# Alternating the column halves of a pair's values, keeping norm chains whole, and idle matmuls in a two-block fp32 kernel

## The chip, the cores and the metric

The kernel runs on one core of one Trainium2 chip. Five engines work in parallel, each with its own instruction stream: TensorE (PE, matmuls; its weight loads are shown apart as PEld), VectorE (DVE), ScalarE (ACT), GpSimd (POOL) and SyncE (SP), which issues most DMAs. TensorE's clock has two levels, 1.2 and 2.4 GHz; the profile shows the granted clock as a share of the full one. The metric is the device time in microseconds of one execution, lower is better, compared as medians of several runs.

## The reference

Two transformer blocks of two layers each work on 256 latent tokens and 256 context tokens of width 1024, in fp32. All of it is matrix products, norms and modulations of this kind:

```python
def ffn_half_step(h, shift, scale, gate, g, w_in, w_out):
    a, b = jnp.split(modulate(rms_norm(h, g), shift, scale) @ w_in, 2, axis=-1)
    return h + FFN_RESIDUAL_WEIGHT * gate * ((jax.nn.silu(a) * b) @ w_out)

# first block, each layer: ffn, mixer1, ffn
q = mla_queries(q_lat, g_q_lat[l], w_q_up[l], g_q_head[l], rope)
k, v = mla_keys_values(kv_lat, k_pe, g_kv_lat[l], w_kv_up[l], g_k_head[l], rope)
kc, vc = mla_keys_values(kv_lat_c, k_pe_c, g_kv_lat[l], w_kv_up[l], g_k_head[l], None)
attn = latent_attention(q, k, v, kc, vc)          # softmax(q k' + ...) v, 8 heads
sg = spatial_gating(sg_in, g_sgu[l], w_spatial[l], b_spatial[l])
cv = short_conv(cv_in, w_conv[l])
h = h + mod_l[5] * merge_groups(attn, sg, cv, g_out[l], w_mix_out[l])

# second block, each layer: mixer2 (an mLSTM group and a neighbourhood attention), then
def sq_relu_mlp(h, w1, w2):
    return jnp.square(jax.nn.relu(h @ w1)) @ w2
```

`mla_queries` and `mla_keys_values` norm a latent (384 or 256 wide), multiply it up to 8 heads of 96, norm each head and rotate 32 of its values. Latent queries attend to all 512 tokens, context queries to the 256 context tokens alone. The last layer of each block needs latent outputs only. Shift, scale and gate come from products of the condition vectors with large modulation weights.

## The kernel before, in words

Activations lie features on partitions: `h[k]`, k = 0 to 7, holds 128 features of 512 tokens, columns 0 to 255 latent (stream 0), 256 to 511 context (stream 1). Each fp32 operand is split into a high and a low part, and each product is three matmuls: high by high, high by low, low by high (`mm_feat`, L340 to L342, tokens as columns; `mm_tok`, L354 to L356, tokens as rows). Weights come in pieces of 1 MB by DMA into three buffers; ScalarE rounds them to the high part (`wh`, L310), VectorE subtracts for the low one (`wl`, L311). Modulation sums (`ad`, L473 and L475) are background work on VectorE: calls of `bg` hand them out, and their weights too come by DMA into these buffers.

The instructions' order on each engine is not the order in the text alone: a planner simulates the program and orders each engine's instructions by its own estimates of when they become due. `issue_after(ins)` limits it: instructions made inside it come behind `ins` where they are on the same engine as `ins`.

A norm has four stages. `Sumsq.add` collects squares feature tile by feature tile as the residual is written: ScalarE squares (L98), VectorE adds (L100), the last tile is squared by VectorE (L103) and kept as a second sum. `rstd_cols` sums over features with narrow matmuls (L552) and runs a chain of eleven small VectorE instructions for the inverse root: L563, L565, then three times two of L570 and one of L571. `rstd_rows` (L546) spreads the factors over partitions by two matmuls. `tile` applies them: VectorE (L133), ScalarE for the high part (`xnh`, L596), VectorE for the low part (`xnl`, L597).

mixer1 makes the latents, norms those of queries (`qs`) and then of keys and values (`kvs`) by `rms_split`, and then multiplies up the queries (L1023, psum `qu`, two halves), keys and values (psum `kvu`). Rotated keys (`kraw`, L873 on VectorE) and queries are transposed per head (psum `tr`, L1135) ahead of attention.

`attention` is a generator over steps, one for each head and query tile of 128: 16 steps per stream. A step makes scores (L807), the row maximum on VectorE (L813), the exponential on ScalarE (L815), the inverse sum and the scaling on VectorE (L817, L818). Three steps later come the transposes of the probabilities (L828), copied by ScalarE (L829) into `pT`, and at each even step the values (L838) of a whole head, for both query tiles: 4 key tiles for latent queries, 2 for context ones. A head's output takes 64 of 128 partitions of a psum tile, so its matmuls use one half of the array's columns (`tile_position=(0, 64 * j)`, j = 0 or 1), and the next head's the other. One fp32 matmul here is two instructions in the trace. Between the steps other generators put in the spatial gating (psum `vs`, L1112, the same kind of halves) and parts of the output projection. mixer2's neighbourhood attention uses the same generator with a bias.

In the second block's mlp, `block` makes three pieces at once at the edge (when both streams are there): `project` multiplies all of stream 0 and then stream 1, ScalarE takes the relu out of psum (L1660), VectorE squares it (L1661) and makes the low part (L594), and `bg` adds modulation sums.

Of the kernel before, what the change touches and what calls it, by code (L numbers as in the profile page):

```python
# [13 lines left out]
ALU = mybir.AluOpType  # L14
AX = mybir.AxisListType

P = 128
D = 1024
KT = 8
# [59 lines left out]
class Sumsq:  # L79


    def __init__(self, b, streams):
        self.b = b
        self.streams = streams
        self.accs = {}

    def add(self, s, k):

        if s not in self.streams:
            return  # L90
        b, nc = self.b, self.b.nc
        ap = b.h[k][:, 256 * s : 256 * s + 256]
        if k == 0:
            self.accs[s] = [b.acc()]
            nc.scalar.activation(self.accs[s][0], ap, AF.Square)
        elif k < KT - 1:
            sq = b.sqtmp()
            nc.scalar.activation(sq, ap, AF.Square)  # L98
            acc = self.accs[s][0]
            nc.vector.tensor_tensor(acc, acc, sq, op=ALU.add)  # L100
        else:
            sq = b.sqtmp()
            nc.vector.tensor_tensor(sq, ap, ap, op=ALU.mult)  # L103
            self.accs[s].append(sq)


class Norm(Sumsq):
# [9 lines left out]
    def emit(self, s):  # L117
        b = self.b
        if s not in self.streams:
            return  # L120
        rb = b.rstd_bc(self.accs[s], D)
        if self.gs is None:
            b.need(self.key, self.sh_chunk)
            b.need(self.key, self.sc_chunk)
            self.gs = b.make_gs(self.key, self.sc_chunk, *self.gain)
        for k in range(KT):
            self.tile(s, k, rb)
# [102 lines left out]
class Builder:  # L230
# [99 lines left out]
    def mm_feat(self, ps, w, m0, x, c0, c1, ks, first, last, kw0=0, m=P):  # L330
        nc = self.nc
        ks = list(ks)
        o = ps[:m, : c1 - c0]
        for i, k in enumerate(ks):
            kw = k - kw0
            st = first and i == 0
            en = last and i == len(ks) - 1
            wh = w.h[:, kw, m0 : m0 + m]
            wl = w.l[:, kw, m0 : m0 + m]
            nc.tensor.matmul(o, wh, x.H(k, c0, c1), start=st, stop=False)  # L340
            nc.tensor.matmul(o, wh, x.L(k, c0, c1), start=False, stop=False)  # L341
            nc.tensor.matmul(o, wl, x.H(k, c0, c1), start=False, stop=en)  # L342


    def mm_tok(self, ps_ap, w, n0, n1, x, t0, ks, first, last, kw0=0):
# [90 lines left out]
    SG0 = 2  # L436
    SG1 = 2
    ML_B = 4

    def ada_tasks(self, blk, l):  # L440

# [92 lines left out]
            v.scalar_tensor_tensor(t, t, -0.5, y, op0=ALU.mult, op1=ALU.mult)  # L534
            v.scalar_tensor_tensor(y, t, 1.5, y, op0=ALU.add, op1=ALU.mult)

    def rstd_bc(self, accs, n):


        return self.rstd_rows(self.psum("nm", "nm"), accs, n)  # L540

    def rstd_rows(self, ps, accs, n):
        nc = self.nc
        y = self.rstd_cols(ps, accs, n)
        for b in range(2):
            self.rows_done = nc.tensor.matmul(ps[:, b * P : (b + 1) * P], y[:, b : b + 1].broadcast_to([P, P]), self.ident, start=True, stop=True)  # L546
        return ps[:, 0:256]

    def token_sums(self, ps, sq, first, last):

        for b in range(2):
            self.nc.tensor.matmul(ps[:, 256 + b : 257 + b], sq[:, b * P : (b + 1) * P], self.onecol,  # L552
                                  start=(first and b == 0), stop=(last and b == 1))

    def rstd_cols(self, ps, accs, n):

        nc = self.nc
        v = nc.vector
        for i, acc in enumerate(accs):
            self.token_sums(ps, acc, i == 0, i == len(accs) - 1)  # L560

        m = self.small(2, "ms", tag="ns")
        v.tensor_scalar(m, ps[:, 256:258], -0.5 / n, -0.5 * EPS, op0=ALU.mult, op1=ALU.add)  # L563
# [3 lines left out]
        for _ in range(3):  # L567
            for b in range(2):
                c = slice(b, b + 1)
                v.scalar_tensor_tensor(t[:, c], y[:, c], m[:, c], y[:, c], op0=ALU.mult, op1=ALU.mult)  # L570
            v.scalar_tensor_tensor(y, t, 1.5, y, op0=ALU.add, op1=ALU.mult)  # L571
        return y

    def sumsq(self, tiles):
# [118 lines left out]
    def ffn(self, l, which, streams, x, nxt, side=None, start=None):  # L693
        nc = self.nc
# [46 lines left out]
        def first_pair():  # L741

            raws = [start.load(0)]
            ws = weights(0)
            raws += [start.load(i) for i in range(1, 4)]
            pp = [[self.psum("fa") for _ in ws] for _ in range(2)]
            for i in range(4):
# [44 lines left out]
    def attention(self, units, nring):  # L792

        nc = self.nc
        ring = [self.arena([P, 2, 1024], F32, "att") for _ in range(nring)]
        st = [(i, qt) for i in range(len(units)) for qt in range(2)]
# [30 lines left out]
            nc.scalar.activation(pT[:, :nk, qt * P : (qt + 1) * P], pt[:, : nk * P].rearrange("p (k q) -> p k q", q=P), AF.Copy)  # L829
            live[i] = pT  # L830

        def values(i):
            q_ap, k_ap, v_ap, po, j, s, bias, done = units[i]
            nk, k0 = (4, 0) if s == 0 else (2, 2)
            pT = live.pop(i)
            o = po()
            for k in range(nk):
                nc.tensor.matmul(o, v_ap(k0 + k), pT[:, k, :], start=(k == 0), stop=(k == nk - 1), tile_position=(0, 64 * j))  # L838
            if done is not None:
                done()  # L840

        n = len(st)
        for e in range(n + 6):
            if e < n:
                scores(*st[e])
            if 3 <= e < n + 3:
                transposes(*st[e - 3])
            if e >= 6 and (e - 6) % 2 == 0 and (e - 6) // 2 < len(units):
                values((e - 6) // 2)
            yield  # L850


# [39 lines left out]

    def rms_split(self, tiles, n, gcol, dst, k0, streams):

        nc = self.nc
        for s in streams:
            c0, c1 = 256 * s, 256 * s + 256
            rb = self.rstd_bc(self.sumsq([t[:, c0:c1] for t in tiles]), n)
            for i, t in enumerate(tiles):
                u = self.ntmp("ru")  # L900
                nc.vector.scalar_tensor_tensor(u, t[:, c0:c1], gcol[:, i : i + 1], rb, op0=ALU.mult, op1=ALU.mult)
                self.split_from(u, dst, k0 + i, c0, c1)

    def mixer1(self, l, last, x, nxt):
        nc = self.nc
# [60 lines left out]
        self.rms_split([kvl[:, i, :] for i in range(2)], 256, self.vec("g_kv_lat", 2 * l, 2), kvs, 0, [0, 1])  # L966


        vgz = self.arena([P, 2048], F32, "vgz")
# [50 lines left out]
        for half in range(2):  # L1020
            w = self.weight(a["w_q_up"][l][:, half * 384 : half * 384 + 384], 3, 384)
            for tt in tts:
# [5 lines left out]
                nc.scalar.activation(sq, ps[:, :384], AF.Square)  # L1028
                o = tt * 8 + 4 * half
                v.tensor_reduce(qss[:, o : o + 4], sq.rearrange("p (h d) -> p h d", d=96), axis=AX.X, op=ALU.add)  # L1030
        kflat, kraw = zip(*[heads("kraw") for _ in range(2)])
        kss = self.small(32, "kss")
        vt = self.arena([P, 4, 512], F32, "vt")
# [93 lines left out]

        qT = [self.arena([P, 4, T], F32, "qT") for _ in range(2)]
        kT = [self.arena([P, 4, T], F32, "kT") for _ in range(2)]
        for h in range(8):  # L1130
            for src, dst, n in ((kflat, kT, 4), (qflat, qT, nt)):
                ps = self.psum("tr")
# [511 lines left out]
    def mlp(self, l, streams, x, nxt):  # L1644
# [8 lines left out]
        def block(t0, edge):  # L1653
# [7 lines left out]
                nc.vector.tensor_tensor(r, r, r, op=ALU.mult)  # L1661
                self.split_from(r, g[t // 8], t % 8 + j, c0, c1)

            self.project(blocks, x, streams, n > 1, range(KT), evac)
            self.bg(n)
            return 2 * n

        def part_in(t0, t1, edge=False):
# [36 lines left out]
    def run(self):  # L1705
# [22 lines left out]
        for l in range(2):  # L1728
# [6 lines left out]
                return  # L1735
            rest = [0] if last else both
            n = norm(0, l, "g_ffn2", 6, rest)
            self.mixer1(l, last, x, n)
            x = n.x
            if self.stop == "h2":  # L1740
# [17 lines left out]
        for l in range(2):  # L1758
            last = l == 1
            rest = [0] if last else both  # L1760
            n = norm(1, l, "norm2_g_2", 3, rest)
            self.mixer2(l, last, x, n)
            x = n.x
            n = Final(self) if last else norm(1, 1, "norm1_g_2", 0, both)
# [64 lines left out]
```

## Time and profile before

| what | value |
| --- | --- |
| three runs | 2982.9, 2988.43, 2988.7 us, median 2988.43 us |
| the profiled execution's own time | 2986.06 us |
| its span in the profile | 2984.3 us |
| mean granted clock of TensorE | 0.988 |
| TensorE busy | 2903.6 us, 97% |
| VectorE busy | 2121.7 us, 71% |
| ScalarE busy | 1088.5 us, 36% |

The span is the stretch that the profile covers; 1.8 us of the execution lie around it. Start times in rows count from the start of the span. A busy share is a mean over stages that have different limits. Instructions of TensorE overlap at their ends, so the distance from start to start tells what one costs, and its duration is longer.

### The profile page before, as it was taken

The numbers are of one execution on the slowest core, as the hardware profiler recorded it, in microseconds if no ns is written. First come the engines' busy times: TensorE is split into PE (matmuls) and PEld (weight loads), VectorE is DVE, ScalarE is ACT, GpSimd is POOL, SyncE is SP. The second block draws the span as 40 slices with busy tenths as digits, with TensorE's granted clock in tenths as the row PEclk, the third lists the DMA queues.
The fourth block names the chain that finished last, engine by engine and source line by source line (L and its number), as shares of the span: only waits on it lengthen the run. The fifth ranks groups of instructions, "written<-read, shape, count | busy, mean of one in ns | idle before, by whom it ended". The sixth has DMA issues, their size and how long they took to land.

```text
span 2984.3 us, 44357 instructions
## 1 busy us (share of the span) xinstructions
PE 2903.6 (97%) x17770; PEld 2484.6 (83%) x17770; DVE 2121.7 (71%) x4323; ACT 1088.5 (36%) x1989; POOL 47.8 (2%) x83
## 2 busy tenths in 40 slices
PE   8999999999999999999988999999999999999998
PEld 6788898688888888888868999886888889995998
DVE  6978768769887697786885675437687875537665
ACT  3222135533222232222653443335342223434443
POOL 0000000000000000000000000011000000011000
PEclk9999999999999999999998999999999999999999
DMA  7655524114655446554323554202255652312453
GB/s 243 216 181 199 171 60 125 47 50 163 216 184 166 140 157 201 179 172 146 107 92 111 175 174 129 75 1 68 85 161 178 198 170 58 118 50 84 155 184 112
DMA packets 357610, 410.25 MB, mean 137 GB/s; under 512 B 24066, under 2 KB 297884, under 8 KB 357404
## 3 DMA queue, kind: packets, MB, share of 16 engines
q1 hardware_dynamic: 353512, 403.63, 41.9%
q10 hardware_dynamic: 3892, 3.78, 0.4%
q8 instruction: 140, 2.29, 0.3%
q14 instruction: 66, 0.54, 0.1%
HBM read 406.34 MB, written 1.05 MB: 137 GB/s over the span
## 4 chain that ended last, share of the span: by engine, by line
PE 91%; DVE 5%; DMA 2%; ACT 1%; issue 1%; SPq 0%; POOL 0%; ACTq 0%; DVEq 0%; POOLq 0%
PE pj L340 13%; PE pj L341 13%; PE pj L342 13%; PE fa L340 9%; PE fa L341 9%; PE fa L342 9%; PE po L838 3%; PE pf L340 2%; PE pf L342 2%; PE pf L341 2%; PE sc L807 2%; DVE wl L311 1%; PE pt L828 1%; PE pj L354 1%; PE pj L355 1%; PE pj L356 1%
## 5 line engine op out<-in xcount | busy, mean ns | idle before, releaser
L310 ACT ACTIVATE wh<-wr 128x1024 fp32r<-128x1024 f32 (+3 forms) x542 | 526.0, 1017 | 858.0 <-PE pj L341 473.3
L311 DVE TENSOR_TENSOR wl<-wr,wh 128x1024 fp32r<-128x1024 f32 (+3 forms) x542 | 624.3, 1175 | 175.3 <-ACT wh L310 173.2
L475 DVE SCALAR_TENSOR_TENSOR ad<-wr,silu,ad 128x512 f32<-128x512 f32 x784 | 548.3, 744 | 17.1 <-DMA wr<-in_w_ada_dram 17.1
L340 PE MATMUL fa<-xnh,wh 128*128 128x512 f32 (+1 forms) x1472 | 520.5, 360 | 5.8 <-ACT xnh L596 4.1
L341 PE MATMUL fa<-xnl,wh 128*128 128x512 f32 (+1 forms) x1472 | 523.1, 357 | 1.9 <-DVE xnl L597 1.9
L342 PE MATMUL fa<-xnh,wl 128*128 128x512 f32 (+1 forms) x1472 | 522.9, 356 | 1.3 <-DVE wl L311 1.3
L340 PE MATMUL pj<-gh,wh 128*128 128x256 f32 (+1 forms) x1372 | 457.2, 334 | 0.0
L342 PE MATMUL pj<-gh,wl 128*128 128x256 f32 (+1 forms) x1372 | 455.7, 333 | 0.0
L341 PE MATMUL pj<-gl,wh 128*128 128x256 f32 (+1 forms) x1372 | 455.5, 332 | 0.0
L340 PEld LDWEIGHTS fa<-xnh,wh 128*128 128x128 f32 x1472 | 275.2, 189 | 52.3 <-ACT xnh L596 5.5
L342 PEld LDWEIGHTS fa<-xnh,wl 128*128 128x128 f32 x1472 | 277.6, 189 | 45.1 <-DVE wl L311 1.7
L341 PEld LDWEIGHTS fa<-xnl,wh 128*128 128x128 f32 x1472 | 277.6, 189 | 43.7 <-DVE xnl L597 2.9
L340 PEld LDWEIGHTS pj<-gh,wh 128*128 128x128 f32 x1372 | 258.7, 189 | 28.3 <-ACT wh L310 1.6
L342 PEld LDWEIGHTS pj<-gh,wl 128*128 128x128 f32 x1372 | 258.5, 188 | 27.2
L341 PEld LDWEIGHTS pj<-gl,wh 128*128 128x128 f32 x1372 | 258.8, 189 | 26.2 <-issue 0.2
L340 PE MATMUL pj<-xnh,wh 128*128 128x256 f32 (+1 forms) x824 | 259.0, 324 | 2.4 <-ACT xnh L596 2.2
L342 PE MATMUL pj<-xnh,wl 128*128 128x256 f32 (+1 forms) x824 | 260.8, 320 | 0.0
L341 PE MATMUL pj<-xnl,wh 128*128 128x256 f32 (+1 forms) x824 | 259.4, 319 | 1.2 <-DVE xnl L597 1.1
L340 PEld LDWEIGHTS pj<-xnh,wh 128*128 128x128 f32 x824 | 155.2, 193 | 14.6 <-ACT xnh L596 3.2
L341 PEld LDWEIGHTS pj<-xnl,wh 128*128 128x128 f32 x824 | 156.5, 191 | 12.6 <-DVE xnl L597 1.4
L342 PEld LDWEIGHTS pj<-xnh,wl 128*128 128x128 f32 x824 | 156.0, 190 | 11.9
L689 DVE SCALAR_TENSOR_TENSOR h<-pj,mod,h 128x256 f32<-128x256 f32 x144 | 66.2, 479 | 109.9 <-PE pj L342 109.9
(372 smaller groups left out, 4260.9 us busy)
## 6 DMA issues: line engine op xcount, KB each, us to landing
wr<-in_w_ada_dram SPq DMA_DIRECT2D x112, 1024.0 KB, 5.2
wr<-in_w_ffn_in_dram SPq DMA_DIRECT2D x88, 1024.0 KB, 5.1
wr<-in_w_mlp_dram SPq DMA_DIRECT2D x64, 1024.0 KB, 5.5
wr<-in_w_ffn_out_dram SPq DMA_DIRECT2D x32, 1024.0 KB, 5.1
wr<-in_w_in_dram SPq DMA_DIRECT2D x20, 1024.0 KB, 5.3
wr<-in_w_ffn_out_dram SPq DMA_DIRECT2D x16, 768.0 KB, 5.4
wr<-in_w_mix_in_dram SPq DMA_DIRECT2D x12, 1024.0 KB, 5.6
ar<-in_w_ada_dram SPq DMA_DIRECT2D x8, 1024.0 KB, 12.6
```

Of the source, the lines that this page charges most:

```text
L310: self.nc.scalar.activation(h[:, i0:i1], raw[:, i0:i1], AF.Copy)
L311: self.nc.vector.tensor_tensor(l[:, i0:i1], raw[:, i0:i1], h[:, i0:i1].bitcast(F32), op=ALU.subtract)
L340: nc.tensor.matmul(o, wh, x.H(k, c0, c1), start=st, stop=False)
L341: nc.tensor.matmul(o, wh, x.L(k, c0, c1), start=False, stop=False)
L342: nc.tensor.matmul(o, wl, x.H(k, c0, c1), start=False, stop=en)
L354: nc.tensor.matmul(ps_ap, xh, w.h[:, kw, n0:n1], start=st, stop=False)
L355: nc.tensor.matmul(ps_ap, xh, w.l[:, kw, n0:n1], start=False, stop=False)
L356: nc.tensor.matmul(ps_ap, xl, w.h[:, kw, n0:n1], start=False, stop=en)
L475: nc.vector.scalar_tensor_tensor(acc[:, j], raw[:, k - k0], s[:, k, j : j + 1], acc[:, j], op0=ALU.mult, op1=ALU.add)
L689: self.nc.vector.scalar_tensor_tensor(self.h[m][:, e0:e1], ps[:, e0 - c0 : e1 - c0], gate[:, m, s : s + 1], self.h[m][:, e0:e1], op0=ALU.m ...
L807: nc.tensor.matmul(ps[:, :w], q_ap(q0), k_ap(k0 * P, (k0 + nk) * P), start=True, stop=bias is None)
L838: nc.tensor.matmul(o, v_ap(k0 + k), pT[:, k, :], start=(k == 0), stop=(k == nk - 1), tile_position=(0, 64 * j))
```

## The change

Five things, in the order of the diff below.

- `Sumsq.add`: with one stream only, the last two feature tiles (not only the last) are squared by VectorE and kept as sums of their own, so three pairs of sums instead of two.
- `busy(n, after)`: n matmuls of the identity by itself into a psum tile of the small-norm pool, behind a given matmul. Two norms get `BUSY = (5, 8, 4)`: five behind the last product before the norm, eight behind the sums, four behind the rows; they are the norms behind the last layer's mixer1 and mixer2. `BUSY_HEADS = 12` stand before the head transposes of the last mixer1.
- `chain_end`, the last instruction of a norm's chain: the low halves of the first weights (start of the kernel), and at the edge of the second block's first mlp the evacuations on VectorE and the modulation sums, are put behind it.
- `attention`: values are issued for a pair of heads, the key tiles in the outer loop and the heads in the inner one, so that neighbours use different column halves; once in four steps, ahead of that step's transposes.
- mixer1: the key latents' sums and chains stay where they were, but rows and application come behind the first half of the query products.

```diff
-        elif k < KT - 1:
+        elif k < KT - (2 if len(self.streams) == 1 else 1):
...
-        rb = b.rstd_bc(self.accs[s], D)
+        idle = self.idle if s == self.streams[-1] else (0, 0, 0)
+        b.busy(idle[0], b.last_mm)
+        rb = b.rstd_bc(self.accs[s], D, idle[1])
+        b.busy(idle[2], b.rows_done)
...
+    BUSY = (5, 8, 4)
+    BUSY_HEADS = 12
...
+    def busy(self, n, after):
+        if n:
+            ps = self.psum("busy", "nm")
+            with self.tc.issue_after(after.ins):
+                for _ in range(n):
+                    self.nc.tensor.matmul(ps[:, :P], self.ident, self.ident, start=True, stop=True)
...
+        self.busy(idle, self.sum_mm)
...
-            v.scalar_tensor_tensor(y, t, 1.5, y, op0=ALU.add, op1=ALU.mult)
+            self.chain_end = v.scalar_tensor_tensor(y, t, 1.5, y, op0=ALU.add, op1=ALU.mult)
...
-            ws = weights(0)
+            with self.tc.issue_after(self.chain_end.ins):
+                ws = weights(0)
...
-        def values(i):
-            q_ap, k_ap, v_ap, po, j, s, bias, done = units[i]
-            nk, k0 = (4, 0) if s == 0 else (2, 2)
-            pT = live.pop(i)
-            o = po()
+        def values(p):
+            pair = units[2 * p : 2 * p + 2]
+            nk, k0 = (4, 0) if pair[0][5] == 0 else (2, 2)
+            pTs = [live.pop(2 * p + j) for j in range(2)]
+            outs = [unit[3]() for unit in pair]
             for k in range(nk):
-                nc.tensor.matmul(o, v_ap(k0 + k), pT[:, k, :], start=(k == 0), stop=(k == nk - 1), tile_position=(0, 64 * j))
-            if done is not None:
-                done()
+                for j, (o, unit) in enumerate(zip(outs, pair)):
+                    nc.tensor.matmul(o, unit[2](k0 + k), pTs[j][:, k, :], start=(k == 0), stop=(k == nk - 1), tile_position=(0, 64 * j))
+            for unit in pair:
+                if unit[7] is not None:
+                    unit[7]()
...
-        for e in range(n + 6):
+        for e in range(n + 4):
             if e < n:
                 scores(*st[e])
+            if e >= 7 and (e - 7) % 4 == 0:
+                values((e - 7) // 4)
             if 3 <= e < n + 3:
                 transposes(*st[e - 3])
-            if e >= 6 and (e - 6) % 2 == 0 and (e - 6) // 2 < len(units):
-                values((e - 6) // 2)
             yield
...
+        self.sums()
+        self.sums()
+        kv_apply = [self.rms_begin([kvl[:, i, :] for i in range(2)], 256, self.vec("g_kv_lat", 2 * l, 2), kvs, 0, s) for s in (0, 1)]
...
+            if half == 0:
+                for apply in kv_apply:
+                    apply()
...
+        if last:
+            self.busy(self.BUSY_HEADS, self.last_mm)
...
-            self.project(blocks, x, streams, n > 1, range(KT), evac)
-            self.bg(n)
+            with self.tc.issue_after(self.chain_end.ins) if n > 1 else nullcontext():
+                self.project(blocks, x, streams, n > 1, range(KT), evac)
+                self.bg(n)
...
             n = norm(0, l, "g_ffn2", 6, rest)
+            if last:
+                n.idle = self.BUSY
...
             n = norm(1, l, "norm2_g_2", 3, rest)
+            if last:
+                n.idle = self.BUSY
```

## Rows read from the trace of the kernel before

**Rows 1.** The page: the chain that ended last, share of the span by engine.

```profile
PE 91%; DVE 5%; DMA 2%; ACT 1%; issue 1%; SPq 0%; POOL 0%; ACTq 0%; DVEq 0%; POOLq 0%
```

**Rows 2.** Waits of PE, whole span: us in total, times, longest.

```profile
PE nm L546 <- DVE rs L571: 21.6, 9, 4.6
...
PE tr L1135 <- DVE kraw L873: 3.3, 1, 3.3
```

**Rows 3.** Windows after norms: length, PE, PEld, DVE, ACT, POOL busy, clock, DMA.

```profile
637.80:641.30 3.50, 3.50 (x17) 3.50 (x18) 3.15 (x7) 1.97 (x6) 0.00 (x0) 0.51 0.26 36
1466.00:1474.00 8.00, 5.70 (x19) 5.41 (x20) 3.84 (x19) 3.54 (x15) 0.00 (x0) 0.58 0.68 225
...
1597.00:1614.00 17.00, 9.40 (x43) 8.82 (x42) 12.98 (x36) 6.35 (x12) 0.00 (x0) 0.60 0.45 147
...
2174.00:2184.00 10.00, 7.04 (x29) 6.46 (x30) 8.16 (x19) 2.76 (x7) 0.00 (x0) 0.50 0.28 102
2780.00:2792.00 12.00, 6.54 (x33) 6.06 (x33) 10.33 (x30) 5.12 (x9) 0.00 (x0) 0.72 0.52 168
```

**Rows 4.** Timeline of PE in the first attention: start, length, instruction.

```profile
558.65 1.94 PE L838 MATMUL po<-att,vt 128*64 128x256 f32 x8
560.52 0.66 PE L828 MATMUL pt<-ident,p 128*128 128x128 f32 x4
561.01 1.02 PE L807 MATMUL sc<-kT,qT 128*128 128x512 f32 x2
561.88 0.38 PE L828 MATMUL pt<-ident,p 128*128 128x128 f32 x2
```

**Rows 5.** Timeline of PE, spatial gating in the same layer.

```profile
546.08 1.97 PE L1112 MATMUL vs<-sg,vgz 128*64 128x128 f32 x32
```

**Rows 6.** Windows of attentions, columns as in rows 3.

```profile
548.00:583.00 35.00, 33.06 (x154) 18.89 (x153) 28.71 (x120) 20.96 (x52) 0.00 (x0) 1.00 0.14 39
583.00:612.00 29.00, 27.97 (x154) 18.92 (x152) 22.22 (x85) 18.16 (x59) 0.00 (x0) 1.00 0.00 1
...
2029.00:2070.00 41.00, 41.00 (x187) 21.84 (x186) 29.99 (x93) 19.44 (x46) 3.55 (x3) 1.00 0.28 71
...
2700.00:2760.00 60.00, 56.94 (x273) 32.66 (x271) 40.55 (x117) 30.74 (x67) 2.78 (x4) 0.97 0.36 102
```

**Rows 7.** Groups of VectorE, 548 to 583: busy us, mean ns, idle before.

```profile
L813 DVE TENSOR_REDUCE nm<-sc 128x1 f32<-128x512 f32 x14 | 9.4, 671 | 0.0
L818 DVE TENSOR_SCALAR p<-p,rinv 128x512 f32<-128x512 f32 x13 | 6.2, 478 | 0.0
L570 DVE SCALAR_TENSOR_TENSOR nt<-rs,ms 128x1 f32<-128x1 f32 x24 | 4.1, 211 | 0.0
```

**Rows 8.** Groups of ScalarE, the same stretch.

```profile
L815 ACT ACTIVATE p<-sc,nm 128x512 f32<-128x512 f32 x13 | 8.9, 685 | 4.6 <-DVE nm L813 3.3 <-DVE rs L571 0.9 <-DVE ms L563 0.3
L829 ACT ACTIVATE att<-pt 128x512 f32<-128x512 f32 x12 | 7.1, 595 | 4.1 <-PE pt L828 3.7
```

**Rows 9.** Timeline of PE at four norms, in brackets the idle time before.

```profile
27.21 1.23 PE L546 MATMUL nm<-ident,rs 128*128 128x128 f32 x4 [4.59 <-DVE rs L571]
...
1468.30 1.22 PE L546 MATMUL nm<-ident,rs 128*128 128x128 f32 x4 [4.13 <-DVE rs L571]
...
1601.71 1.01 PE L552 MATMUL nm<-sumto,acc 128*128 128x1 f32 x4 [4.29 <-DVE acc L100]
...
1605.77 1.22 PE L546 MATMUL nm<-ident,rs 128*128 128x128 f32 x4 [2.19 <-DVE rs L571]
...
2174.73 1.22 PE L546 MATMUL nm<-ident,rs 128*128 128x128 f32 x4 [3.75 <-DVE rs L571]
2177.06 1.44 PE L340 MATMUL pj<-xnh,wh 128*128 128x256 f32 x5 [1.11 <-ACT xnh L596]
```

**Rows 10.** Timeline of VectorE, first mlp of the second block: chain's ends.

```profile
2164.30 0.16 DVE L563 TENSOR_SCALAR ms<-nm 128x2 f32<-128x2 f32 x1 [1.10 <-PE nm L552]
...
2174.52 0.15 DVE L571 SCALAR_TENSOR_TENSOR rs<-nt,rs 128x2 f32<-128x2 f32 x1
```

More of the change, by code (lines that the diff above doesn't have):

```diff
@@ L79 @@
 class Sumsq:
+    idle = (0, 0, 0)
     def __init__(self, b, streams):
@@ L341, in mm_feat @@
             nc.tensor.matmul(o, wh, x.L(k, c0, c1), start=False, stop=False)
-            nc.tensor.matmul(o, wl, x.H(k, c0, c1), start=False, stop=en)
+            self.last_mm = nc.tensor.matmul(o, wl, x.H(k, c0, c1), start=False, stop=en)
     def mm_tok(self, ps_ap, w, n0, n1, x, t0, ks, first, last, kw0=0):
@@ L535, in rsqrt_small, with rstd_bc, rstd_rows @@
             v.scalar_tensor_tensor(y, t, 1.5, y, op0=ALU.add, op1=ALU.mult)
-    def rstd_bc(self, accs, n):
-        return self.rstd_rows(self.psum("nm", "nm"), accs, n)
-    def rstd_rows(self, ps, accs, n):
+    def busy(self, n, after):
[4 more added lines that the diff above has]
+                    self.nc.tensor.matmul(ps[:, :P], self.ident, self.ident, start=True, stop=True)
+    def rstd_bc(self, accs, n, idle=0):
+        ps = self.psum("nm", "nm")
+        return self.rstd_rows(ps, self.rstd_cols(ps, accs, n, idle))
+    def rstd_rows(self, ps, y):
         nc = self.nc
-        y = self.rstd_cols(ps, accs, n)
         for b in range(2):
@@ L551, in token_sums, with rstd_cols @@
         for b in range(2):
-            self.nc.tensor.matmul(ps[:, 256 + b : 257 + b], sq[:, b * P : (b + 1) * P], self.onecol,
-                                  start=(first and b == 0), stop=(last and b == 1))
-    def rstd_cols(self, ps, accs, n):
+            self.sum_mm = self.nc.tensor.matmul(ps[:, 256 + b : 257 + b], sq[:, b * P : (b + 1) * P], self.onecol,
+                                                start=(first and b == 0), stop=(last and b == 1))
+    def rstd_cols(self, ps, accs, n, idle=0):
         nc = self.nc
@@ L893, in rms_split, with rms_begin, apply @@
     def rms_split(self, tiles, n, gcol, dst, k0, streams):
+        for s in streams:
+            self.rms_begin(tiles, n, gcol, dst, k0, s)()
+    def rms_begin(self, tiles, n, gcol, dst, k0, s):
         nc = self.nc
-        for s in streams:
-            c0, c1 = 256 * s, 256 * s + 256
-            rb = self.rstd_bc(self.sumsq([t[:, c0:c1] for t in tiles]), n)
+        c0, c1 = 256 * s, 256 * s + 256
+        ps = self.psum("nm", "nm")
+        y = self.rstd_cols(ps, self.sumsq([t[:, c0:c1] for t in tiles]), n)
+        def apply():
+            rb = self.rstd_rows(ps, y)
             for i, t in enumerate(tiles):
@@ L902, in rms_split @@
                 self.split_from(u, dst, k0 + i, c0, c1)
+        return apply
     def mixer1(self, l, last, x, nxt):
@@ L965, in mixer1 @@
         kvs = Split(self, 2, "kvs", per=2, joint=True)
-        self.rms_split([kvl[:, i, :] for i in range(2)], 256, self.vec("g_kv_lat", 2 * l, 2), kvs, 0, [0, 1])
+        self.sums()
+        self.sums()
+        kv_apply = [self.rms_begin([kvl[:, i, :] for i in range(2)], 256, self.vec("g_kv_lat", 2 * l, 2), kvs, 0, s) for s in (0, 1)]
         vgz = self.arena([P, 2048], F32, "vgz")
```

## The prediction

> **What bounds the kernel now.** I read the page first: TensorE (PE) holds 91% of the chain that ended last, VectorE (DVE) 5% [rows 1]. So two things pay: fewer PE microseconds, or fewer PE waits. The waits of PE come next: matmuls that spread a norm's factors over the partitions (L546) and wait for the norm's chain on VectorE are the largest item, 21.6 us in 9 waits; the key transposes (L1135) wait 3.3 us [rows 2]. Last the table by windows: after such waits the granted clock is 0.50 to 0.72 of full speed, that is 1.2 GHz instead of 2.4 for all or part of the stretch [rows 3]. A gap of some microseconds is paid twice, as a wait and as slow matmuls behind it.
>
> **Part 1, values of a pair.** One head's values are 8 instructions of 256 columns on one column half: 1.94 us, 1.87 up to the next start, 234 ns each [rows 4]. Before, a head's eight share a half, and the next head's eight share the other; after, neighbours alternate. The nearest row for alternating halves is the spatial gating, whose j alternates too: 32 instructions of 128 columns in 1.97 us, 62 ns each [rows 5]. On the full array an instruction of 128 columns takes 0.12 us (four transposes, 0.49 us up to the next score [rows 4]), so two halves run side by side at nearly no loss. A pair of heads over four key tiles then goes from 3.74 us to 16 instructions at twice 62 ns, 2.0 us; with some overhead I take 1.6 us as saved. Bounds: 0 (halves don't overlap) and 1.9 (half of the time). Four attentions with 4 such pairs each give 16 x 1.6 = 25.6 us; the two layers that keep the context have 8 more pairs over two key tiles, at 0.8 us 6.4. Together 32 us.
>
> What does each attention give of it? It ends with the later of TensorE and VectorE. In the first attention's latent half TensorE is busy 33.06 of 35 us and VectorE 28.71 [rows 6]: 1.15 us a step of softmax (maximum 0.67, scaling 0.48 [rows 7]), and the norms of the side branches. Less 6.4, TensorE needs 26.7, less than VectorE, which works without a break only if nothing is late for it: I take 3.5 of 6.4. In the context half VectorE has 22.22 of 29: 2.5 of 3.2. Later attentions have more room, 29.99 of 41 and 40.55 of 60 [rows 6]: 7.5 of 9.6 in mixer2's first layer, and 4.5 of 6.4 in each last layer. Sum 6 + 7.5 + 4.5 + 4.5 = **22.5 us**; ends 8 (rival a) and 32.
>
> Values also move ahead of the transposes of their step, so the copy of the transposes before (0.60 us on ScalarE [rows 8]) has only the next scores to hide behind (0.87 us from the scores' start to that of the transposes [rows 4]), where a step's transposes lay between as well. It is hidden if ScalarE takes it at once; behind an exponential (0.69 us [rows 8]) it comes 0.69 + 0.60 - 0.87 = 0.4 us late, and with the handing over between engines some 0.6 us. I count this in the share not taken above.
>
> **Part 2, chains kept whole.** At the start PE waits 4.59 us for the chain of the context stream [rows 9], among whose steps VectorE splits weights. The modulation matmuls that follow wait for their weights, which come by DMA and not sooner, so most of the wait moves there: **1.5 us** (0 to 2.5, half of the wait and a little). In the second block's first mlp the chain runs from 2164.30 to 2174.67 [rows 10], as modulation sums, squares and low halves stand between its steps. Left alone it is six steps of 0.21 us [rows 7] and five shorter ones, an estimate of 2.2 us. So its rows are ready before PE's latent products end, 3.75 us before it gets them now; then it waits 1.11 us for the first tile [rows 9], and for 10 us it runs at half clock, where 7.04 us of matmuls could take 3.5 [rows 3]. All of it is 3.75 + 1.11 + 3.5 = 8.4 us. What is late next: the squares and low halves that queue behind the chain, and the modulation sums with the DMA buffers that they hold, on an engine already busy 8.16 of those 10 us [rows 3]. PSUM is not held, as ScalarE reads it out. I take **7 us** (4 to 8.4).
>
> **Part 3, key factors behind the queries.** In the last mixer1 PE waits 4.13 us for rows of the key latents [rows 9], and its clock is 0.58 in these 8 us [rows 3]. The query products need none of it and may start 4.13 + 1.22 = 5.4 us earlier, at full clock (up to 5.70/2 = 2.8 more). But this stage ends with PE waiting 3.3 us for the rotated keys [rows 2], VectorE's work, and VectorE is idle in only 4.2 of the 8 us [rows 3]: what it can't do earlier comes back as that wait. In the first layer I saw no wait there. **5 us** (2 to 8).
>
> **Part 4, idle matmuls, and one square more on VectorE.** An idle matmul is two instructions of 128 columns, 0.25 us; 17 are 4.2 us, and the waits of mixer1's last norm are 4.29 + 2.19 = 6.5 us [rows 9], so they lie in waits. If they hold the clock, what runs there at half (17 us at 0.60 with 9.40 busy [rows 3]) gains up to 4.3; I take 3, as tiles must still come from VectorE. The seventh square on VectorE takes ScalarE out of the sums' way: 0.5. Together **3.5 us** (-1 to 5: the five after the last product can stand in front of the sums). In mixer2's last norm the clock is 0.72 over 12 us with PE busy 6.54 and VectorE 10.33 [rows 3]; VectorE would set the pace: **2 us** (0 to 3). Twelve before the head transposes are 3.0 us, under the wait of 3.3 [rows 2]; VectorE's and ScalarE's copies bound the transposes: **0.5 us** (-1 to 1). The last norm of all gets the square too; I count nothing, as it trades one ScalarE square and one addition for four short sums.
>
> **Sum.** 22.5 + 1.5 + 7 + 5 + 3.5 + 2 + 0.5 = 42 us, from the profiled execution's 2986.06: 2944. That execution is 0.1% under the median of 2988.43 and inside the three runs; with most of this difference, **2946**. All lower ends together give 12, all upper 60.
>
> **Rivals.** (a) *ScalarE's copy is late in every pair.* 24 pairs x 0.6 us take 14.4 of the 22.5 back, which leaves 8 and 27.5 in all: 2960. For it: exponential and copy are both due after the same scores, and the exponential waits for VectorE's maximum. Against: ScalarE is busy only 20.96 of 35 us [rows 6]. (b) *The halves don't overlap.* Attention gives nothing, the rest 19.5: 2968. Against: the gating's 62 ns [rows 5]. The Trainium skill ("TensorE: Matmul & The Clock Gate", The mechanism) says that a weight load overlaps matmuls in flight only where the row group differs, and the two halves share theirs; by that rule the loads would end the overlap, and the time would be that of (b). The trace disagrees: the gating's 32 products are on such halves, and took 1.97 us, loads included. (c) *The other side: gaps in attention drop the clock.* A pair whose values wait leaves a gap, and a stretch of 3.5 us at half clock (637.80: 3.50 busy at 0.51 [rows 3]) costs 1.7 us. If all 24 pairs fell, 24 x 1.7 = 41 stand against 8 + 19.5: +13, 3000. It decides from 16 such pairs. Against: the first attention runs at 1.00, though with idle PE time of 1 to 2 us in each window, and the last one at 0.97 [rows 6]. The page named above (A second HAM failure mode: psum-queue depth-cycling) tells of frequent short idles that make the clock swing; that is this case, and the trace bears it out only behind single waits so far. (d) *Idle matmuls don't hold the clock, and the keys come when they came.* Parts 3 and 4 give 2 instead of 11: 33 in all, 2954.
>
> **How the numbers follow.** Forecast 0.65, (a) 0.14, (b) 0.06, (c) 0.07, (d) 0.08. The forecast's own span is 2930 to 2960. The range, 2930 to 2966, takes in (a) and (d), and leaves out (b), (c) and a tail of the forecast of 0.06. Changes within 0.2%, about 6 us, can't be told from none. All cases but (c) are faster by more, and of (c) a third ends near no change: faster 0.93, same 0.02, slower 0.05.
>
> **What would show it.** Values as pairs a few ns apart, and PE's busy time down by 25 to 32 us but for the idle matmuls and the clock; each attention shorter by the share above, at 1.00; no wait of 3.75 us near 2175, and 1.00 there; the waits of L546 down from 21.6 us to under 10; query products ahead of the key rows; the two last norms at full clock, their sums no later. The prediction is wrong if attention keeps its length while VectorE or ScalarE fills, if values wait for the copy in each pair, if half-clock stretches appear inside attention, or if the wait at L1135 grows by what the queries gained.

## The result, and the profile after

The changed kernel takes 2956.62 us (median of 2948.49 to 2961.51, 4 runs) against 2988.15 us: a ratio of 0.9896, 95% interval 0.987 to 0.9921, so about 31 us less. Its profiled execution took 2955.05 us (span 2953.3). The forecast was 2946, range 2930 to 2966.

I lay both traces side by side by landmarks of TensorE's work, and take the lengths between them. A first matmul counts from its start, a last one to its end:

| stage, between landmarks on PE | before | after | difference | forecast |
| --- | --- | --- | --- | --- |
| start, to the end of the first `fa` products | 384.14 | 383.73 | -0.41 | -1.5 |
| mixer1, first layer: first score to last value | 76.28 | 68.25 | -8.03 | -6 |
| mixer1, last layer: latents done to first key transpose | 54.18 | 53.89 | -0.29 | -5 |
| key transposes, to the first score | 9.73 | 8.18 | -1.55 | -0.5 |
| mixer1, last layer: first score to last value | 47.33 | 41.90 | -5.43 | -4.5 |
| then to the first product of the feed-forward, and to its last `fa` | 214.29 | 212.43 | -1.86 | -3.5 |
| mixer2, first layer: first score to last value | 142.31 | 134.88 | -7.43 | -7.5 |
| first mlp, to the last modulation matmul | 368.74 | 366.64 | -2.10 | -7 |
| mixer2, last layer: first score to last value | 94.90 | 94.01 | -0.89 | -4.5 |
| from there to the first transpose of the outputs (7.6 us before the end) | 216.76 | 212.76 | -4.00 | -2 |

Together these stages give 32 us, and the two spans differ by 31; all other stages together lose 1. The first score of mixer2 belongs to its mLSTM group, which comes ahead of the neighbourhood attention. What the rows show:

The chain that ended last (page), and PE's waits over the whole span: us in total, times, longest.

```profile
PE 91%; DVE 5%; ACT 2%; DMA 1%; issue 1%; SPq 0%; POOL 0%; ACTq 0%; DVEq 0%; POOLq 0%
```

```profile
PE nm L562 <- DVE rs L588: 7.3, 5, 2.9
PE tr L1173 <- DVE kraw L894: 6.2, 1, 6.2
```

TensorE still bounds the kernel [rows 1]. Waits for norm chains went from 21.6 to 7.3 us, and the wait for the rotated keys doubled from 3.3 to 6.2 [rows 2]. The twelve idle matmuls hide another 2.8 us of this wait (experiment 3 shows it without them).

Timeline of PE in the first attention, to lay beside [rows 4]:

```profile
565.96 1.95 PE L858 MATMUL po<-att,vt 128*64 128x256 f32 x16
567.84 0.66 PE L847 MATMUL pt<-ident,p 128*128 128x128 f32 x4
```

A whole pair now takes 1.88 us up to the next start, what one head took before. But in 6 of the 16 pairs over four key tiles, and in 6 of the 8 over two, the planner put other matmuls, often a norm's, behind the first of the pair:

```profile
574.96 0.65 PE L858 MATMUL po<-att,vt 128*64 128x256 f32 x2
575.54 0.71 PE L562 MATMUL nm<-ident,rs 128*128 128x128 f32 x4
576.18 1.94 PE L858 MATMUL po<-att,vt 128*64 128x256 f32 x14
```

Such a pair takes 0.65 + 1.94 = 2.6 us, and so saves 1.3 us where a whole one saves 1.9. The next view is the table by windows for the values' tile alone, its last line, which sums the four attentions (540 to 630, 1510 to 1575, 2020 to 2115 and 2690 to 2760; length, then PE's busy time on the tile), of the kernel before and then of the changed one:

```profile
sum 320.00, PE 82.29 PEld 40.90 DVE 9.71 ACT 4.21; mean PE 20.57 PEld 10.23 DVE 2.43 ACT 1.05
```

```profile
sum 320.00, PE 49.99 PEld 24.06 DVE 10.10 ACT 4.58; mean PE 12.50 PEld 6.02 DVE 2.52 ACT 1.15
```

82.3 - 50.0 = 32.3 us of PE time went; the forecast had 32. The windows of the attentions (columns as in [rows 3]), and then those around the norms:

```profile
545.00:580.00 35.00, 33.01 (x199) 19.68 (x198) 32.64 (x130) 24.53 (x62) 0.00 (x0) 1.00 0.14 39
580.00:604.00 24.00, 22.64 (x143) 15.94 (x142) 18.94 (x77) 17.22 (x58) 0.00 (x0) 1.00 0.00 1
...
2052.00:2088.00 36.00, 32.69 (x191) 20.55 (x191) 23.66 (x66) 23.70 (x66) 0.00 (x0) 1.00 0.29 89
2697.00:2735.00 38.00, 35.95 (x196) 20.92 (x196) 26.25 (x68) 22.71 (x47) 1.38 (x2) 0.91 0.46 148
```

```profile
1453.00:1466.00 13.00, 11.04 (x64) 10.03 (x62) 11.84 (x35) 10.54 (x28) 0.00 (x0) 1.00 0.74 227
...
1583.00:1596.00 13.00, 12.29 (x90) 11.97 (x89) 11.08 (x33) 4.74 (x8) 0.00 (x0) 0.87 0.63 204
...
2147.00:2158.00 11.00, 8.65 (x54) 8.22 (x58) 10.81 (x25) 3.97 (x9) 0.00 (x0) 0.69 0.12 33
2755.00:2770.00 15.00, 13.58 (x113) 13.20 (x113) 9.68 (x30) 5.16 (x11) 0.00 (x0) 1.00 0.26 75
2663.00:2670.10 7.10, 7.10 (x30) 6.56 (x31) 4.07 (x11) 2.84 (x8) 1.24 (x2) 0.52 0.00 1
```

In the first attention VectorE is now busy 32.64 of 35 us, TensorE 33.01: the two limits meet [rows 6]. At the query products the clock is 1.00 where it was 0.58, at the two last norms 0.87 and 1.00 where it was 0.60 and 0.72 [rows 3]. At the first mlp's norm it is 0.69 where it was 0.50, not the 1.00 that was forecast. But 2663 to 2670, in the mLSTM part of the last layer's mixer2, is new at half clock. From the first score of the neighbourhood attention to the last value that layer takes 52.08 us against 56.20, 4.1 less; the mLSTM part ahead of it takes 41.9 against 38.7, 3.2 more. That part takes 38.7 to 39.1 us in the six profiles on record without this half-clock stretch and 41.9 in the six with it, so the 3.2 us go with the clock, and this is why the whole stage shows only 0.89 us. The mean granted clock is 0.988 in both profiles: half-clock time went at the norms and came back elsewhere.

### The profile page after: what moved, and what is told of

It reads as the page before. It is cut to its first block, busy times and chain, and to the rows that moved or that the text cites. A ratio compares the mean times of both kernels' runs of the same rounds, so it can differ in the third digit from the quotient of the medians.

```text
span 2953.3 us, 44554 instructions
## 1 busy us (share of the span) xinstructions
PE 2885.5 (98%) x17874; PEld 2480.1 (84%) x17874; DVE 2122.6 (72%) x4323; ACT 1086.5 (37%) x1986; POOL 47.8 (2%) x83
## 4 chain that ended last, share of the span: by engine, by line
PE 91%; DVE 5%; ACT 2%; DMA 1%; issue 1%; SPq 0%; POOL 0%; ACTq 0%; DVEq 0%; POOLq 0%
PE pj L346 14%; PE pj L347 13%; PE pj L348 13%; PE fa L346 9%; PE fa L347 9%; PE fa L348 9%; PE pf L346 2%; PE pf L348 2%; PE pf L347 2%; PE sc L826 2%; PE po L858 1%; DVE wl L317 1%; PE pj L360 1%; PE pj L361 1%; PE pj L362 1%; PE pt L847 1%
```

## The experiments

Each edit is to the changed kernel unless said otherwise. The 4 or 5 runs of a kernel scatter by up to 17 us, so the stages above decide, each from one profile, and the medians only where they are clear of this.

**1. The values alone.** The kernel before, with `attention` of the changed kernel and nothing else:

```diff
-            if e >= 6 and (e - 6) % 2 == 0 and (e - 6) // 2 < len(units):
-                values((e - 6) // 2)
+            if e >= 7 and (e - 7) % 4 == 0:
+                values((e - 7) // 4)
```

> The kernel before with the new values of a pair alone (alternating halves, ahead of the transposes). Theory 1, the halves run side by side: the four attentions become shorter by about 8.4, 5.4, 7.8 and 5.7 us as between the two traces, 27 us in all, so about 2961. Rival, the gain needs the other parts (whole chains and idle matmuls keep the clock up): under 20 us, above 2968.

Measured 2968.71 us (2961.04 to 2971.08), ratio 0.9932 [0.9914, 0.995]: 18 us less than before. Stage by stage: mixer1's attentions 68.25 and 42.03 us, as in the changed kernel, mixer2's 140.83 and 91.33. Mixer2's first has a half-clock stretch of 17 us from 2069.6, which neither kernel of the two traces has. The four softmax attentions alone (from their own first score) take 18.8 us less, against 25.1 in the changed kernel, and the 6 us between the two are mixer2's first. So the median is at the rival's number, the mechanism is there in full, and the clock took part of it back. That the other parts would have kept the clock up is not shown: the kernels of experiments 8 and 9 have them, and show such a stretch there too.

**2. No alternation.**

```diff
-            for k in range(nk):
-                for j, (o, unit) in enumerate(zip(outs, pair)):
+            for j, (o, unit) in enumerate(zip(outs, pair)):
+                for k in range(nk):
```

> The changed kernel, but each pair's values head by head (heads in the outer loop, key tiles in the inner), at the same place in the step. Theory 1: all that the alternation saved comes back, PE busy in attention up by 25 to 32 us, the time up by 20 to 30 us to about 2980. Rival, the new place (once in four steps, ahead of the transposes) brought the gain: within 5 us of the changed kernel. A third reading, the place costs something by itself: more than 30 us come back, over 2987.

Measured 2964.95 us (2964.36 to 2966.03), ratio 0.9927 [0.9912, 0.9942]: only 8 us over the changed kernel, and neither reading as I put it. The four softmax attentions take 14.0 us longer than in the changed kernel. The values' tile by windows, as above, and a pair in the timeline of PE:

```profile
sum 320.00, PE 69.33 PEld 37.53 DVE 10.15 ACT 4.60; mean PE 17.33 PEld 9.38 DVE 2.54 ACT 1.15
```

```profile
566.75 2.86 PE L858 MATMUL po<-att,vt 128*64 128x256 f32 x16
```

Two heads issued one behind the other take 2.86 us, not 2 x 1.94. The sixteen starts within that row tell why: four come alone, about 0.22 us apart, from 566.75; then four pairs, 0.01 to 0.06 us apart, from 567.66; then four alone again. In the program the eight of one head stand ahead of the eight of the next, so I read this as the second head beginning when three of the first one's are still to start, on the half of the columns that is free. That is a gain of 1.0 us of the 1.9 for a pair that stands together. In this kernel only 10 of the 16 pairs over four key tiles, and 3 of the 8 over two, do; between the others' heads the planner put other matmuls, and each head then takes what it took before. So 82.3 - 69.3 = 13 us of the 32 come without alternation, in this placing, and 69.3 - 50.0 = 19 with it; how much would come without it if all pairs stood together, no run shows.

**3. No idle matmuls.** `BUSY = (0, 0, 0)`, `BUSY_HEADS = 0`.

> The changed kernel without idle matmuls. Theory 1, they hold the clock only at the two norms: the stretch behind mixer1's last norm returns to half clock and costs 2 to 3 us, the one behind mixer2's last norm 3 us, the head transposes nothing (their twelve ended 6 us before the keys came): 5 us more, about 2962. Rival, they do nothing and the seventh square alone made these norms shorter: no change, norms at the same clock as with them.

Measured 2956.93 us (2950.45 to 2966.21), ratio 0.9902 [0.9876, 0.9928]. The windows at the two last norms, and then in mixer2's first attention:

```profile
1589.00:1602.00 13.00, 9.34 (x50) 8.96 (x51) 9.02 (x29) 3.74 (x8) 0.00 (x0) 0.61 0.28 90
2759.00:2772.00 13.00, 8.10 (x42) 7.72 (x43) 10.51 (x29) 4.56 (x9) 0.00 (x0) 0.61 0.39 122
```

```profile
2058.00:2103.00 45.00, 43.15 (x209) 26.96 (x208) 23.39 (x64) 22.18 (x61) 0.00 (x0) 0.77 0.22 71
```

```profile
PE tr L1173 <- DVE kraw L894: 9.2, 1, 9.2
```

The last line is PE's wait for the rotated keys over the whole span. At both norms the clock is 0.61 again. From the last value to the first product of the feed-forward nothing changes (35.05 against 35.18 us), its products take 179.52 against 177.25, and the tail 215.27 against 212.76: 4.8 us in the two places. At the two norms the idle matmuls do what they are for. The key transposes take 7.90 against 8.18: the twelve there do nothing, since PE still waits 9.2 us for the keys without them. The stage ahead of the transposes is 1.8 us longer here (55.73), but so it is in experiments 7 and 8 (55.7 and 55.6), which have the twelve. The medians are equal all the same. In these two profiles the clock's part goes both ways: mixer2's first stage, at 0.77 in its context half, takes 7.6 us more, and its last layer 3.5 less. Two executions of this kernel, 2950.5 and 2951.0, are faster than three of the four of the changed kernel, so that the idle matmuls shorten the whole program is not shown.

**4. Keys first.** Rows and application of the key latents ahead of the query products, as before.

```diff
-            if half == 0:
-                for apply in kv_apply:
-                    apply()
```

> The changed kernel with the key latents' rows and application ahead of the query products again. Theory 1, the 6 us that the query products gained were lost again at the key transposes: the wait of 6.2 us at the transposes falls to about 3, the wait for rows of 4 us is back, and the time differs by less than 3 us. Rival, the move is worth its 5 us: 5 us more.

Measured 2955.49 us (2950.65 to 2958.15), ratio 0.9893 [0.9879, 0.9908]. From the latents to the first score: 53.21 + 9.59 = 62.80 us, against 53.89 + 8.18 = 62.07 in the changed kernel and 63.91 in the kernel before. The wait for the rows is back, up to 4.1 us, and that at the transposes falls to 0.63 behind the twelve idle matmuls, 3.5 us with them:

```profile
1505.79 0.66 PE L1168 MATMUL tr<-ident,kraw 128*128 128x128 f32 x4 [0.63 <-DVE kraw L894]
```

By these numbers the move is worth 0.7 us: theory 1. Even this is not clear of the scatter: the six profiles that have the move and not experiment 6's order lie between 61.2 and 63.6 us.

**5. Chains open.** Both `issue_after(self.chain_end.ins)` taken out.

> The changed kernel without the two orders that put work behind the end of a norm's chain. Theory 1, whole chains help the edge of the first mlp by 2 to 3 us and the start not at all, since the start's 3.5 us were given back in a wait at 88 us: 2 to 3 us more than the changed kernel, all between 2130 and 2160. Rival, they are worth the 8.5 us that were forecast, and another part took them back: 7 us or more.

Measured 2954.07 us (2951.33 to 2955.48), ratio 0.9885 [0.9871, 0.9898]: no slower. The start takes 385.64 against 383.73 us and the first mlp 368.75 against 366.64: 1.9 and 2.1 us. For the mlp theory 1 holds, and other profiles bear it out: the three kernels with open chains take 368.3 to 368.8 us for this stage, the nine with closed ones 366.1 to 367.2. At the start the 1.9 us are within the scatter: kernels with the same start as the changed one take 381.9 to 387.3 us. The median doesn't tell 4 us from none. Why so little? Timeline of VectorE in the first mlp of the changed kernel:

```profile
2136.24 0.16 DVE L580 TENSOR_SCALAR ms<-nm 128x2 f32<-128x2 f32 x1 [3.93 <-PE nm L568]
...
2138.29 1.41 DVE L483 SCALAR_TENSOR_TENSOR ad<-wr,silu,ad 128x512 f32<-128x512 f32 x2
...
2142.32 0.16 DVE L588 SCALAR_TENSOR_TENSOR rs<-nt,rs 128x2 f32<-128x2 f32 x1
2142.40 1.76 DVE L1699 TENSOR_TENSOR r<-r 128x256 f32<-128x256 f32 x5
2144.07 1.41 DVE L483 SCALAR_TENSOR_TENSOR ad<-wr,silu,ad 128x512 f32<-128x512 f32 x2
2145.40 1.08 DVE L611 TENSOR_TENSOR gl<-r,gh 128x256 fp32r<-128x256 f32 x3
2146.41 1.25 DVE L139 SCALAR_TENSOR_TENSOR nt<-h,gs,nm 128x256 f32<-128x256 f32 x3
```

The chain is not whole: it takes 6.2 us, because modulation sums that were made elsewhere, and so not inside `issue_after`, still run between its steps. Then PE waits not for rows but for the tiles: their first step on VectorE (L139) stands behind the squares (L1699), sums and low halves (L611) that were held back:

```profile
2147.47 1.09 PE L346 MATMUL pj<-xnh,wh 128*128 128x256 f32 x5 [2.37 <-ACT xnh L613]
2150.44 0.58 PE L347 MATMUL pj<-xnl,wh 128*128 128x256 f32 x1 [1.88 <-DVE xnl L614]
```

**6. Keys whole.** In the last mixer1 the last convolution's read-out, the gating's start and the output projection stand behind the last instruction of the rotation (`head_end`, the addition in `head_scale`).

```diff
+            with self.tc.issue_after(self.head_end.ins) if last and f0 == 1184 else nullcontext():
+                self.project([(w, [0, P], None)], x, streams, False, range(KT), ev)
...
+        with self.tc.issue_after(self.head_end.ins) if last else nullcontext():
+            next(sgating)
...
+        with self.tc.issue_after(self.head_end.ins) if last else nullcontext():
+            for _ in out:
+                pass
```

> The changed kernel, and in the last mixer1 the last convolution's read-out, the gating's start and the output weights' low halves stand behind the end of the key rotation on VectorE. Theory 1, the query products' gain was lost because VectorE put other work into the key rotation: the wait of 6.2 us at the key transposes falls to about 2, and the stage ends some 4 us earlier, the time 3 to 5 us lower. Rival, the stage is bound by VectorE's sum of work: the wait goes, and the 4 us come back as waits in the attention that follows.

Measured 2946.26 us (2938.19 to 2948.28), ratio 0.9855 [0.984, 0.9869]. From the latents to the first score 47.46 + 11.00 = 58.46 us, 3.6 less than in the changed kernel, and the attention behind it is not longer (40.47 against 41.90). The two kernels of experiments 9 and 10, which have the same order, take 60.3 us, with attentions of 38.8. The timeline of VectorE of the changed kernel, and then of this one:

```profile
1503.07 0.68 DVE L883 TENSOR_TENSOR kraw<-kraw,blk 128x512 f32<-128x512 f32 x1
1503.67 2.35 DVE L317 TENSOR_TENSOR wl<-wr,wh 128x1024 fp32r<-128x1024 f32 x2
...
1506.33 0.68 DVE L894 TENSOR_TENSOR kraw<-rope,rope 128x512 f32<-128x512 f32 x1
```

```profile
1494.44 0.68 DVE L883 TENSOR_TENSOR kraw<-kraw,blk 128x512 f32<-128x512 f32 x1
1495.05 0.41 DVE L910 SCALAR_TENSOR_TENSOR gq<-gq,pj 128x256 f32<-128x256 f32 x1
1495.38 0.68 DVE L894 TENSOR_TENSOR kraw<-rope,rope 128x512 f32<-128x512 f32 x1
1495.98 0.87 DVE L1111 SCALAR_TENSOR_TENSOR yB<-vgz,cols,yB 128x255 f32<-128x255 f32 x2
1496.77 0.41 DVE L1137 TENSOR_REDUCE vm<-vsq 128x4 f32<-128x256 f32 x1
1497.10 4.62 DVE L317 TENSOR_TENSOR wl<-wr,wh 128x1024 fp32r<-128x1024 f32 x4
```

Two splits of output weights, needed only behind the attention, stood between the last two steps of the rotation. With the rotation ahead of them the keys are ready at 1496.06, before PE is, and the wait for them is gone. Timeline of PE in this kernel:

```profile
1496.50 2.84 PE L551 MATMUL busy<-ident 128*128 128x128 f32 x24
1499.18 0.60 PE L1175 MATMUL tr<-ident,kraw 128*128 128x128 f32 x4
...
1502.27 0.66 PE L1175 MATMUL tr<-ident,kraw 128*128 128x128 f32 x4 [1.27 <-DVE yB L912]
```

The rival is right in part: some of the work that was moved back now makes the transposes wait for VectorE in between, and they take 11.00 us against 8.18. And the twelve idle matmuls no longer lie in a wait: they stand between ready keys and the transposes. No run leaves them out here, so what they cost is open.

**7. Head by head in the context streams**, alternation for the latents alone (`nk == 4`).

> The changed kernel with pairs of the context streams issued head by head, those of the latents alternating. Theory 1 (gaps in attention drop the clock, where the products are small): the half-clock stretch of 17 to 20 us that some executions show in mixer2's context attention goes, and the times of the executions lie within 5 us of each other, against 13 us; the median is at or under the changed kernel's. Rival, the clock's fall there has nothing to do with the alternation: spread as before, and 2 to 3 us more for the values.

Measured 2955.91 us (2945.91 to 2961.49), ratio 0.9882 [0.9867, 0.9898]. The times scatter by 15.6 us, and the profile has a half-clock stretch of 13.7 us from 2062.7 in that attention, where the heads do not alternate. My theory that alternating there makes the clock fall is refuted.

**8. Vectors apart.** `load_vectors` takes its psum tile from the small-norm pool in its second call.

> The changed kernel, with the second load of small vectors in a psum buffer of the small-norm pool instead of one of the five for products. Theory 1, the start's gain of 3.5 us was lost because the vectors' transposes waited for a product buffer at 85.9 to 87.7 us, and the clock fell after it: both go, and the first layer ends 3 us earlier. Rival, the wait only moves to the next product, whose buffer is freed by the same instruction on VectorE: no change.

Measured 2950.02 us (2943.35 to 2956.55), ratio 0.9872 [0.9855, 0.9889]. The start takes 379.56 us against 383.73, 4.2 less. In the changed kernel the start's gain was lost here:

```profile
24.36 1.22 PE L562 MATMUL nm<-ident,rs 128*128 128x128 f32 x4 [2.94 <-DVE rs L588]
...
87.72 0.26 PE L415 MATMUL pv<-ident,rows 48*128 48x48 f32 x1 [1.83 <-DVE th L741]
88.64 0.47 PE L346 MATMUL fa<-xnh,wh 128*128 128x512 f32 x1 [0.66 <-DVE cols L416]
```

The last of four transposes waits for a psum tile of the products' pool until VectorE has read it out, and a half-clock stretch of 3.4 us begins at 89.7. With a tile of its own both are gone. Not all of the 4.2 us are the wait's: three kernels with the same start and a wait of 1.4 to 1.5 us have no half-clock stretch there (experiments 3, 4 and 6) and take 381.9 to 382.6, while the kernels with the tile of its own take 379.6 to 380.3. So I put the wait at about 2 us, an estimate, and the rest down to the clock.

**9 and 10. Both of these together, and both with four idle matmuls** in the one PE wait (0.88 us) ahead of the place where the clock falls in mixer2's first attention.

> The changed kernel with the key rotation kept whole and the second load of vectors in the small-norm pool. Theory, the two mend different stages and add: 3.6 us at the keys and about 3 at the start below the changed kernel, and what the clock does besides: 2942 to 2948, and under the changed kernel by more than 0.2%. Rival, one of the two single gains was only the clock's: no better than the key rotation alone.

> The kernel of the run before it, and four idle matmuls (0.9 us) in the one wait of PE of 0.88 us in the context half of mixer2's first attention. Theory, that wait is what lets the clock fall there in some executions: no half-clock stretch there, times of the executions closer together, the median at or under the run before. Rival, the wait does not decide (the changed kernel has it and kept its clock): stretches of 14 to 20 us still in some executions, spread as before.

Measured 2943.64 us (2938.17 to 2955.32), ratio 0.985 [0.9832, 0.9868], the lowest of all, though not clear of experiment 6; and 2947.07 us (2938.22 to 2948.63), ratio 0.9856 [0.9837, 0.9875]. Without the idle matmuls the attention's stage takes 140.53 us with 17 us at half clock, with them 137.58 with 6.8, beginning after the next wait, of 0.80 us. One profile each doesn't settle it. The wait in question, in the changed kernel and in that of experiment 1:

```profile
2059.15 0.70 PE L826 MATMUL sc<-knT,qnT 64*128 64x256 f32 x2 [0.88 <-ACT p L834]
```

```profile
2067.02 0.70 PE L808 MATMUL sc<-knT,qnT 64*128 64x256 f32 x2 [0.89 <-ACT p L816]
```

Behind the first the clock stayed at 1.00; behind the second it fell at 2069.6.

## Why the prediction was right, and where its terms were off

*Values of a pair.* The mechanism and PE's saving, 32 us, were right: 32.3 measured. The sum is in part luck: a pair over four key tiles saved 1.9 or 1.3 us, on average about 1.7 where I took 1.6, and one over two key tiles about 0.6 where I took 0.8 (estimates from the lengths of the pairs). What the attentions gave of it was forecast at 22.5, and the stages measure 8.03 + 5.43 + 7.43 + 0.89 = 21.8. Within this, two errors cancel. The softmax attentions alone gave 8.0 + 5.4 + 7.5 + 4.1 = 25.1. Where the clock stayed the same they gave more than I took (20.9 against 18 in the first three), so I had put too much of the saving down to VectorE; the last one gave 4.1 against 4.5. The mLSTM part ahead of that last one took back 3.2 us at half clock, which no term of the sum has. And the step "a pair goes from 3.74 us to 2.0 because neighbours alternate" gave alternation all of the gain: 13 of the 32 us come already without it, where two heads stand next to each other.

*Chains kept whole.* Mis-sized: 8.5 forecast, about 2.5 measured (4 in experiment 5, of which the mlp's 2.1 are clear of the scatter). The step "left alone it is six steps and five shorter ones, an estimate of 2.2 us" failed, as the order covers only what is made inside it: 10.4 us became 6.2, not 2.2. The step on what is late next, the squares and low halves, came true and cost 2.37 and 1.88 us at once. At the start the gain was 3.5 us by the start of the same product at 72 us, and lost from 88 on, in a wait that the prediction doesn't have and the half clock behind it.

*Key factors behind the queries.* Mis-sized: 5 forecast, 0.7 measured, which is not clear of none. The products did start 6 us earlier and at full clock; the prediction's last paragraph named the wait at the key transposes as the place where this can be lost, and it was: with the idle matmuls out it is 9.2 us against 3.3, so it grew by 5.9, what the queries had gained. This sign of being wrong came true. I took VectorE's idle 4.2 us to be filled by the keys' chain. It was not, as other work was put between its steps; experiment 6 put 3.6 us of it back (1.8 in the profiles of experiments 9 and 10).

*Idle matmuls.* 6 forecast; 4.8 measured by taking them out, and 5.9 in the two stages together with the seventh square. That is two stages in one profile; the medians show nothing of it. The larger part is at mixer2's norm, not at mixer1's (4.0 and 1.9 us in the table); the twelve before the key transposes are worth nothing.

*Rivals.* (a) did not come: 21.8 of 22.5. (b) is refuted by the row of 16 in 1.95 us, with 16 weight loads of 0.13 to 0.14 us in the same stretch; so the sentence of the Trainium skill ("TensorE: Matmul & The Clock Gate", The mechanism) by which loads overlap only across row groups doesn't hold here. (c) came in part: of the ten profiles in which latent pairs alternate, six (that of experiment 7 among them) have 7 to 20 us at half clock inside mixer2's first attention, and the kernel before and that without alternation, one profile each, have none there; the four runs of the latter lie within 1.7 us, those of the changed kernel within 13. That stage takes 134.9 us in the four without, and up to 142.4 in the six, so it costs 2.7 to 7.6 us where it comes, and never decided the sign. In all six the clock falls 0.3 to 2.7 us behind the start of the first matmul after a PE wait of 0.80 to 0.89 us; the kernel before and that without alternation have no wait over 0.4 us at that place. So the wait goes with the fall, but does not decide it: the other four, the changed kernel's among them, have the same wait of 0.88 us and kept their clock. What decides stays open. (d) is half true: the clock held at the norms, the keys came when they came.

*The whole.* The terms gave 32 of 42 us: the chains 6.0 less than forecast, the keys and their transposes 3.7 less, the values 0.7 less, the two norms with idle matmuls 0.4 more. The range held since it was wide enough for this, not because each term was right.

## What to carry to other kernels

An order that holds work back behind a chain covers only what is made inside it; look in the trace for what else stands between the chain's steps, and count the work held back as the next wait. A gain on the bounding engine is worth what the next join lets through: here the query products' 6 us needed the key rotation to move too, and one more order gave 1.8 to 3.6 of them. Where the clock of a stretch falls in some executions and not in others, time a change by stages and over several profiles: here one stage moved by 7.6 us with the clock alone.

## What the runs showed of the hardware

- Two products on different column halves overlap even when they are not issued alternately: eight instructions of one head issued ahead of eight of the next took 2.86 us, not 3.88, with starts that come in pairs over the middle half. Issued alternately the sixteen took 1.95.
- The same stretch is found at full and at half clock in programs that differ only elsewhere. In the changed kernel's profile mixer2's first attention ran at 1.00 throughout; without idle matmuls, which stand elsewhere, its context half was at 0.77, with the same wait of 0.88 us ahead of the fall.
- What half clock cost there: that stage took 134.9 us in four profiles at full clock, 137.6 with 6.8 us at 1.2 GHz, 140.5 and 140.8 with 17.1, and 142.0 and 142.4 with 20.5.
